# The second layer's token mixer on pairs of 2-byte floats in place of pairs of 4-byte floats

## The chip, the core and the metric

The kernel runs on one core of one Trainium2 chip. The core has five engines that each take their instructions from a queue of their own, in order: TensorE (PE in the profile, its weight loads PEld), VectorE (DVE), ScalarE (ACT), GpSimd (POOL) and SyncE (SP, which here only issues DMAs). They meet through semaphores. Operands of a matmul come from SBUF (128 partitions), its result goes to PSUM, which has eight banks of 128 x 512 4-byte floats. The metric is the time of one execution on the device in microseconds (us); the median of several runs counts.

## What is computed

Two layers of an encoder, 1024 tokens of 1024 numbers. Each layer normalises its input, shifts and scales it by a conditioning vector, runs a token mixer, adds the gated result, and then does the same with a squared-ReLU MLP. Layer 0's mixer is a latent attention. Layer 1's mixer, the one that the change touches, is a dilated sliding-window attention in three groups of 16 heads of 64:

```python
proj = (h @ w_in).reshape(B, S, 3, 3, 16, 64)          # group, (q k v), head
for gi, (window, dilation) in enumerate(((128, 1), (512, 4), (2048, 16))):
    q = rms_norm(proj[:, :, gi, 0], g_q[gi])
    k = rms_norm(proj[:, :, gi, 1], g_k[gi])
    v = proj[:, :, gi, 2]
    s = q @ k.T * 64 ** -0.5 + bias_table[bucket]       # |i - j| <= window / 2, same residue mod dilation
    o, lse = softmax(s) @ v, logsumexp(s)
wts = softmax(stack(lses), axis=0)                      # over the three groups
y = (sum over groups of wts * o) @ w_o
```

Everything is 4-byte float in the reference.

## The kernel before

**Products of pairs.** The kernel holds each operand of these products as a sum of two numbers, a high part and a low part, and a product is three matmuls: high by high, high by low, low by high (`mm3`, L504 to L506). There are two kinds of pair. `split` (L133, L134) makes two 4-byte numbers (written as fp32r): ACT copies the source into the high part, DVE takes source minus high. `parts` (L148, L151) makes two 2-byte floats: ACT writes the scaled source into the high part, DVE the rest, and that instruction also sums the rest over each row into a column of the tile `seen`. Before the change the two MLPs use `parts`, both mixers `split`.

**The range check.** 2-byte floats hold a small range of sizes, so `seen` collects the sums, and `floor` adds sums of a first tile that must not be too small; `fold` reduces `seen` once after each MLP and `verdict` compares at the end. `program` then runs the whole kernel a second time, on 4-byte pairs throughout (`half` false), if the comparison fails. `hs`, `ws`, `us` and `ys` are powers of two by which h, the weights, the MLP's hidden values and the gate are scaled.

**Layer 1's mixer.** `dil_v` first computes v for all three groups, by blocks in seven products in place of eight; its matmuls write the tile psv and have 512 columns. Then `dil` runs 96 steps, 32 for each group, four for each pair of heads. A step on PE is, in this order: products of q and k for two tiles of 128 queries (`products`, L2013, tile pss; two heads run side by side on 64 rows each); 24 projection matmuls for q and k of one token tile (psproj, 256 columns, `project`); four transposes (`stacks`, L1988, psq); 24 more; and the products of weights and v for two tiles (`av`, L2086 and L2087, psav). v is in three 2-byte parts of 64 columns, the weights of the softmax in two, so a key block costs one matmul of 192 columns and one of 128; groups 0 and 1 have two key blocks for each tile and head, group 2 one.

Around them, for the step just projected: `qkstep` squares (ACT, dsq), sums (DVE, dms), takes a reciprocal root (`rstd`, L124 to L128, ending in dry), multiplies (DVE, qn) and applies the gains (POOL, L1979). Two steps later PE transposes qn and ACT and DVE make the pair kT out of the bank (L1992, L1993). One step after that come the products; DVE adds the bias (L2029), ACT exponentiates (L2035) and makes the high part ph (L2072), DVE or POOL the low part (L2073), SP issues a DMA that transposes both into pT (L2074), and one step later `av` uses pT; DVE adds the three parts of the result into U (L2088). `v_parts` (L1959 to L1962) makes the three parts of v: ACT the first, DVE the rest, POOL the second and third. In group 2 the results of the three groups are merged as well (DVE and POOL, L2157, L2159), transposed, split and stored to a scratch tensor in DRAM, oTd. Before groups 1 and 2 `permute` copies h into the group's order.

Then `proj_res` multiplies with w_o (tile psy, 512 columns) and adds the residual.

**What sets the order.** The program is written in the order above; a scheduler with a model of the engines then orders each queue, and inside `dil` PE's order is held as written. Tiles come from pools of equal buffers (`G`: 29 buffers of 4 KB a partition; `X`: 20 in this layer; `sm`: six of each small size; eight PSUM banks), and a tile whose buffer is still read waits.

Of the kernel before, what the change touches and what calls it, by code (L numbers as in the profile page):

```python
# [41 lines left out]
class K:  # L42
    def __init__(self, ctx, tc, a, half, ng=29):
# [4 lines left out]
        self.hs, self.ws, self.us = (16.0, 512.0, 2.0 ** -10) if half else (1.0, 1.0, 1.0)  # L48
        self.ys = 2.0 ** -15 if half else 1.0
        self.cp = ctx.enter_context(tc.tile_pool(name="const", bufs=1))  # L50
# [6 lines left out]
        if half:  # L57
            misc = self.C("misc", [P, 8])
            self.bad, self.ones_y = misc[:, 0:4], misc[:, 4:5]
# [36 lines left out]
    def DR(self, shape, name):  # L96
        return self.dp.tile(list(shape), F32, name=self.pre + name)


    def setup(self):  # L100
# [6 lines left out]
        if self.half:  # L107
            nc.vector.memset(self.ones_y, self.ys)
        self.mods = {}
# [8 lines left out]
    def rstd(self, ms, n, name):  # L118
# [5 lines left out]
        nc.scalar.activation(l, ms, AF.Ln, bias=self.eps)  # L124
        nc.scalar.activation(y, l, AF.Exp, scale=-0.5)
        nc.vector.scalar_tensor_tensor(t, ms, EPS, y, op0=ALU.add, op1=ALU.mult)
# [9 lines left out]
    def pair(self, alloc, name, shape):  # L136

        if self.half:
            g = alloc(name, (shape[0], 2) + tuple(shape[1:]), F16)
            return g[:, 0], g[:, 1]  # L140
        return tuple(alloc(name + k, shape) for k in "hl")
# [12 lines left out]
    def seen_open(self):  # L154

        if self.half:
            self.seen, self.nseen, self.nlow = self.G("seen", (P, 512), F32), 0, 508
# [8 lines left out]
    def fold(self, k):  # L166

        tr, s = self.nc.vector.tensor_reduce, self.seen
        tr(self.bad[:, k : k + 1], s[:, 0 : self.nseen], op=ALU.add, axis=AX.X, apply_absolute_value=True)
        tr(self.bad[:, k + 2 : k + 3], s[:, 509 : self.nlow + 1], op=ALU.min, axis=AX.X)  # L170

    def verdict(self):

        nc = self.nc
        self.fold(1)
        t, m = self.sm("verdict", 4), self.sm("verdict", 1)
        nc.vector.tensor_scalar(t[:, 0:2], self.bad[:, 0:2], 512.0, None, op0=ALU.is_le)
        nc.vector.tensor_scalar(t[:, 2:4], self.bad[:, 2:4], 128.0, None, op0=ALU.is_ge)
# [41 lines left out]
    def consts(self, psp):  # L220
# [7 lines left out]
        if self.half:  # L228
            b = self.colc[:, 0:96].rearrange("p (l x) -> p l x", l=2)[:, :, 24:32]
            nc.gpsimd.tensor_scalar(b, b, self.hs, 1.0, op0=ALU.mult, op1=ALU.mult)  # L230
            g = self.colc[:, 112:128]
            nc.gpsimd.tensor_scalar(g, g, self.hs, 1.0, op0=ALU.mult, op1=ALU.mult)
# [55 lines left out]
    def ada_col(self, l, s, c, n, ps):  # L288
# [7 lines left out]
        if s == 3 and self.half:  # L296
# [12 lines left out]
    def ada_end(self, l, s, acc, row, psp, tag):  # L309
# [3 lines left out]
        if s % 3 == 2:  # L313
            for h in range(2):
                ps, c = PS(), slice(h * 512, (h + 1) * 512)
                if s == 5 and self.half:
# [91 lines left out]
    def h_store(self, Hh, d, x, mods, act=False, alloc=None, pin=False, keep=None):  # L408
# [3 lines left out]
        if d % 2 == 0:  # L412
            for k in range(2):
                Hh[k].append((alloc or self.G)(f"hT{k}", (P, 2, 512)))
# [12 lines left out]
        self.split(Hh[0][d // 2][:, d % 2, :], Hh[1][d // 2][:, d % 2, :], t)  # L427

    def h_steps(self, xs, mods, alloc=None, halloc=None, pin=False, act=False, keep=None):
# [5 lines left out]
        for d in range(ND):  # L435
            steps.append(lambda psp, tag, d=d: self.h_store(Hh, d, self.xT(xh, d, psp, tag), mods(), act=act or pin and d % 2 == 0,
                                                            alloc=halloc, keep=keep))
# [76 lines left out]

    def wsplit(self, src, shape, name, row=None, gain=None, alloc=None):

        nc = self.nc
        raw = self.load(src, shape, name + "r")
        hi, lo = ((alloc or self.G)(name + k, shape) for k in "hl")
        if row is not None:  # L520
            nc.gpsimd.tensor_tensor(raw, raw, row, op=ALU.mult)
        if gain is not None:
            nc.scalar.activation(hi, raw, AF.Copy, scale=gain)
            nc.vector.scalar_tensor_tensor(lo, raw, gain, hi.bitcast(F32), op0=ALU.mult, op1=ALU.subtract)
        else:
            self.split(hi, lo, raw)
        return hi, lo

# [537 lines left out]
    def reload(self, O, src, pp, th, eng=None):  # L1066
# [1466 lines left out]
```

## Time and profile before

| | |
|---|---|
| median of 3 runs | 3170.82 us (3169.37 to 3176.19) |
| the profiled execution | 3175.89 us |
| its span, first to last instruction | 3174.0 us |
| granted clock of PE, mean | 0.987 |
| v projection of layer 1 (`dil_v`) | from about 1390 to 1635 us of the span |
| the loop of `dil`, groups 0, 1, 2 | from about 1635, 1900 and 2180 us to about 2460 |
| output projection of layer 1 | from about 2460 to 2585 us |
| MLPs | from about 820 to 1390 and from 2585 to the end |

A row of a group of instructions names the line, the engine, the operation, what it writes and what it reads (`out<-in`, buffer numbers left out), partitions x elements and type, and the count; after the bar come the time that the group was busy, the mean of one in ns, and the idle time of the engine just before, with what ended it. "f32" stands for 4-byte operands, the pairs of `split` among them. A row of the order of time has the start and the length in us. A row of a table of stretches has the stretch, its length, each engine's busy time with its count, the granted clock, the DMA share and GB/s.

### The profile page before, as it was taken

What the parts mean: (1) busy time and instruction counts of PE and PEld (TensorE: products, weight loads), DVE (VectorE), ACT (ScalarE), POOL (GpSimd) and SP (SyncE); (2) the same over time, 40 slices, a digit from 0 to 9 for tenths busy, and PEclk for the clock granted to TensorE, in tenths of its full rate; (3) what the DMA queues carried; (4) which work ended last, traced back from release to release, by engine and by line L of the source; (5) the groups of instructions that cost most, each with busy time, mean ns of one, the idle gap of its engine ahead of it and who ended that gap; (6) DMA issues with size and microseconds to landing.
All of it is one profiled execution on the core that took longest, in us unless ns stands there. A gap on an engine that the chain in (4) does not pass through costs nothing. (4 is left out here: it accounts for less than half of the span.)

```text
span 3174.0 us, 51216 instructions
## 1 busy us (share of the span) xinstructions
PE 3072.2 (97%) x18036; PEld 2165.6 (68%) x18036; DVE 2385.7 (75%) x4734; ACT 1726.4 (54%) x3507; POOL 918.5 (29%) x1228
## 2 busy tenths in 40 slices
PE   6999999999999999999999999999999999999998
PEld 6877677778444444457889998999999764444443
DVE  5677777756998876688757778778787689779665
ACT  5547777863545543443226677668565355555441
POOL 7454655630011100001124445444454001110010
PEclk8999999999999999999999999999999999999999
DMA  5352332244665679555637887878776747438653
GB/s 196 110 184 83 108 98 97 71 137 133 215 227 181 240 233 298 190 190 178 212 118 188 181 180 174 193 186 173 168 177 163 217 134 249 163 136 289 226 198 94
DMA packets 540027, 554.53 MB, mean 175 GB/s; under 512 B 199493, under 2 KB 421106, under 8 KB 539754
## 3 DMA queue, kind: packets, MB, share of 16 engines
q1 hardware_dynamic: 501962, 445.10, 49.1%
q0 software_dynamic: 27360, 91.31, 7.8%
q10 hardware_dynamic: 10432, 14.68, 1.6%
q8 instruction: 146, 2.39, 0.3%
q14 instruction: 127, 1.04, 0.1%
HBM read 378.27 MB, written 132.62 MB: 161 GB/s over the span
## 5 line engine op out<-in xcount | busy, mean ns | idle before, releaser
L504 PE MATMUL psm<-hf,wf 128*128 128x512 f16 x896 | 340.8, 380 | 5.1 <-ACT wf L148 5.1
L505 PE MATMUL psm<-d,d 128*128 128x512 f16 x896 | 340.4, 380 | 4.7 <-DVE d L151 4.7
L505 PE MATMUL psm<-hf,wf 128*128 128x512 f16 x896 | 341.1, 381 | 0.0
L506 PE MATMUL psm<-d,d 128*128 128x512 f16 x896 | 340.3, 380 | 0.0
L506 PE MATMUL psm<-hf,wf 128*128 128x512 f16 x896 | 335.4, 381 | 4.7 <-DVE wf L151 4.6
L504 PE MATMUL psm<-d,d 128*128 128x512 f16 x896 | 334.7, 380 | 0.3 <-ACT d L148 0.3
L504 PE MATMUL psproj<-wqkh,hTp 128*128 128x256 f32 x1024 | 304.2, 297 | 0.0
L505 PE MATMUL psproj<-wqkl,hTp 128*128 128x256 f32 x1024 | 292.1, 285 | 0.0
L506 PE MATMUL psproj<-wqkh,hTp 128*128 128x256 f32 x1024 | 291.7, 285 | 0.0
L148 ACT ACTIVATE d<-ufr 128x1024 f16<-128x1024 f32 x112 | 117.8, 1052 | 206.2 <-PE psm L506 172.2
L504 PEld LDWEIGHTS psproj<-wqkh,hTp 128*128 128x128 f32 x1024 | 198.8, 194 | 9.0 <-issue 1.6
L505 PEld LDWEIGHTS psproj<-wqkl,hTp 128*128 128x128 f32 x1024 | 199.1, 194 | 0.2 <-DVE wqkl L134 0.2
L506 PEld LDWEIGHTS psproj<-wqkh,hTp 128*128 128x128 f32 x1024 | 198.5, 194 | 0.0
L151 DVE SCALAR_TENSOR_TENSOR d<-ufr,d 128x1024 f16<-128x1024 f32 x112 | 136.7, 1220 | 80.7 <-ACT d L148 80.5
L835 DVE TENSOR_REDUCE mx<-pmx 128x1 f32<-128x512 f32 x256 | 165.0, 682 | 27.9 <-PE pmx L833 27.7
L134 POOL TENSOR_TENSOR pl<-p,ph 128x1024 fp32r<-128x1024 f32 x58 | 141.3, 2436 | 138.4 <-ACT ph L133 128.2
L947 ACT ACTIVATE p<-pss 128x512 f32<-128x512 f32 x256 | 144.5, 589 | 51.7 <-PE pss L934 50.6
L1979 POOL TENSOR_TENSOR qn<-qn,dgain 128x256 f32<-128x256 f32 x96 | 89.8, 935 | 285.2 <-DVE qn L1977 238.3
L2035 ACT ACTIVATE pd<-pd,dnb 128x192 f32<-128x192 f32 (+2 forms) x384 | 167.7, 438 | 3.7 <-ACT dnb L2033 2.1
L2088 DVE TENSOR_REDUCE U<-psav 128x128 f32<-128x384 f32 x192 | 103.1, 551 | 86.4 <-PE psav L2087 86.1
L506 PEld LDWEIGHTS <-wf 128*128 128x128 f16 x896 | 88.0, 98 | 114.4 <-DVE wf L151 9.0
L504 PEld LDWEIGHTS <-wf 128*128 128x128 f16 x896 | 87.9, 98 | 113.6 <-ACT wf L148 9.6
(428 smaller groups left out, 8805.5 us busy)
## 6 DMA issues: line engine op xcount, KB each, us to landing
ufr<-uf SPq DMA_DIRECT2D x112, 512.0 KB
adaw<-in_ada_w SPq DMA_DIRECT2D x96, 512.0 KB
w2r<-in_mlp_w SPq DMA_DIRECT2D x96, 512.0 KB
w1r<-in_mlp_w SPq DMA_DIRECT2D x64, 512.0 KB
bt<-bias SPq DMA_DIRECT2D x128, 256.0 KB
wqkr<-in_dil_w_in SPq DMA_DIRECT2D x96, 256.0 KB
wvr<-in_dil_w_in SPq DMA_DIRECT2D x34, 512.0 KB
qkv<-st SPq DMA_DIRECT2D x32, 512.0 KB
```

The costliest lines, as they stand in the source:

```text
L134: return (lo_eng or nc.vector).tensor_tensor(lo, src, hi.bitcast(F32), op=ALU.subtract)
L148: nc.scalar.activation(hi, src, AF.Copy, scale=scale)
L151: return nc.vector.scalar_tensor_tensor(lo, src, scale, hi, op0=ALU.mult, op1=ALU.subtract, accum_out=self.seen[:, self.nseen - 1 : self.n ...
L504: mm(out, lh, rh, start=first, stop=False)
L505: mm(out, lh, rl, start=False, stop=False)
L506: mm(out, ll, rh, start=False, stop=last)
L835: nc.vector.tensor_reduce(maxes[h][:, 2 * j + b : 2 * j + b + 1], ps, op=ALU.max, axis=AX.X)
L947: nc.scalar.activation(p[:, b * 512 : (b + 1) * 512], ps[b], AF.Exp)
L1979: nc.gpsimd.tensor_tensor(qq, qq, gain[:, g : g + 1, :].unsqueeze(1).broadcast_to([P, 2, 2, 64]), op=ALU.mult)
L2035: nc.scalar.activation(p[:, e, lo:hi], p[:, e, lo:hi], AF.Exp, bias=nb[:, e : e + 1], accum_out=stat[:, g, t, 1, 2 * pr + e : 2 * pr + e + 1])
L2088: nc.vector.tensor_reduce(u["U"][:, t, :].rearrange("p (e d) -> p e d", e=2), ps[:, 0:384].rearrange("p (e k d) -> p e d k", e=2, k=3), op ...
```

## The change

In layer 1's mixer every `split` becomes a `parts`: h and its sums (hT, hs, hk), the weights wv, wqk and wo, the merged result oT; the pair kT is made on 2-byte floats too, scaled by 64, and v becomes a pair in place of three parts. Products keep their count but for `av`, whose matmuls have 128 and 64 columns in place of 192 and 128. The scales move through the mixer: h by 16, weights by 512, scores by 4096 (bias table and exponentials follow), gates by 2^-15. A pair lies in one buffer of `G` or `X` where two were needed, oTd has half the bytes, and `permute` copies 2-byte numbers. The range check grows: `seen` is opened three times and folded three times, `floor` looks at five first tiles more, and for the norms three small instructions on POOL add up the fourth power of dry in a tile `most`. Layer 0's mixer stays as it was.

```diff
@@ wo_form (w_form, dil_weights.split, h_form, h_store alike)
-        hi, lo = (self.G("wo" + k, (P, 2, 512)) for k in "hl")
-        self.split(hi, lo, raw)
+        half = self.half and self.layer == 1
+        hi, lo = self.pair(alloc or self.G, "wo", (P, 2, 512), half)
+        (self.parts(hi, lo, raw, self.ws) if half else self.split(hi, lo, raw))
@@ v_parts
-            vs = D_("vs", (P, 2, 4, 192), BF16, 8)
+            vs = D_("vs", (P, 2, 4, 128 if self.half else 192), F16 if self.half else BF16, 8)
...
+            if self.half:
+                self.held(lambda: self.parts(v4[:, :, 0:64], v4[:, :, 64:128], p4, 2.0 ** -7))
+                for i in range(n):
+                    VS[t + i] = vs[:, i]
+                return
@@ qkstep
-            r = self.rstd(ms, 8, "dr")
+            r = self.rstd(ms, 8, "dr", self.half)
+            if self.half:
+                y4 = self.sm("y4", 8)
+                nc.gpsimd.tensor_tensor(y4, r, r, op=ALU.mult)
+                nc.gpsimd.tensor_tensor(y4, y4, y4, op=ALU.mult)
+                nc.gpsimd.tensor_tensor(most, most, y4, op=ALU.add)
@@ stacks
-            nc.scalar.activation(hi, x, AF.Copy)
-            nc.vector.tensor_tensor(lo, x, hi.bitcast(F32), op=ALU.subtract)
+            if self.half:
+                nc.scalar.activation(hi, x, AF.Copy, scale=64.0)
+                nc.vector.scalar_tensor_tensor(lo, x, 64.0, hi, op0=ALU.mult, op1=ALU.subtract)
...
@@ av
+                    if self.half:
+                        o = ps[:, e * 128 : (e + 1) * 128]
+                        c = slice((n * e + b) * P, (n * e + b + 1) * P)
+                        nc.tensor.matmul(o, pT[:, 0, c], v, start=b == 0, stop=False)
+                        nc.tensor.matmul(o[:, 0:64], pT[:, 1, c], v[:, 0:64], start=False, stop=b == n - 1)
+                        continue
...
+            k = 2 if self.half else 3
             nc.vector.tensor_reduce(u["U"][:, t, :].rearrange("p (e d) -> p e d", e=2),
-                                    ps[:, 0:384].rearrange("p (e k d) -> p e d k", e=2, k=3), op=ALU.add, axis=AX.X)
+                                    ps[:, 0 : 128 * k].rearrange("p (e k d) -> p e d k", e=2, k=k), op=ALU.add, axis=AX.X)
@@ dil
-        oTd = self.DR([6, 2, P, 2, 512], "oTd")
+        oTd = self.DR([6, 2, P, 2, 512], "oTd", F16 if self.half else F32)
...
-                                      "k": D_("kT", (P, 2, S + 512), F32R, 2), "U": self.G("U", (P, 8, P), F32)}
+                                      "k": D_("kT", (P, 2, S + 512), self.DT, 2), "U": self.G("U", (P, 8, P), F32)}
@@ run
+        k.layer = 1
+        k.seen_open()
         vd = k.DR([3, S, D], "v")
...
         O, first, banks = k.dil(at, at1, tail, wqk, vd)
+        k.fold(1)
+        k.seen_open()
```

How the queues stand at three places. First PE, at the end of a step of group 1, where weights (pT) are multiplied with v (vs). Before:

```order
L2086 LDWEIGHTS pT_23655
L2086 MATMUL psav_23884<-vs_22802,pT_23655 128x192
L2087 LDWEIGHTS pT_23655
L2087 MATMUL psav_23884<-vs_22802,pT_23655 128x128
L2086 LDWEIGHTS pT_23655
L2086 MATMUL psav_23884<-vs_22942,pT_23655 128x192
```

And after the change:

```order
L2109 LDWEIGHTS pT_23640
L2109 MATMUL psav_23868<-vs_22777,pT_23640 128x128
L2110 LDWEIGHTS pT_23640
L2110 MATMUL psav_23868<-vs_22777,pT_23640 128x64
L2109 LDWEIGHTS pT_23640
L2109 MATMUL psav_23868<-vs_22918,pT_23640 128x128
```

The sequence and the number of weight loads are the same; the columns are fewer. Second DVE, in a step of group 2 in which v is split and weights are split (wqk): from the end of the bias additions to the two reductions of U. Before:

```order
L126 SCALAR_TENSOR_TENSOR drt_31781<-dms_31776,dry_31779 128x8
L127 SCALAR_TENSOR_TENSOR drt_31781<-drt_31781,dry_31779 128x8
L134 TENSOR_TENSOR wqkl_31797<-wqkr_31279,wqkh_31796 128x1024
L128 SCALAR_TENSOR_TENSOR dry_31779<-drt_31781,dry_31779 128x8
L134 TENSOR_TENSOR wqkl_31801<-wqkr_31571,wqkh_31800 128x1024
L1977 TENSOR_TENSOR qn_31787<-psproj_31707,dry_31779 128x512
L1960 TENSOR_TENSOR vr_31791<-vraw_31385,vs_31790 128x512
L1993 TENSOR_TENSOR kT_31391<-psq_31869,kT_31391 128x2x256
L2088 TENSOR_REDUCE U_30835<-psav_31900 128x128
L2088 TENSOR_REDUCE U_30835<-psav_31906 128x128
```

And after the change:

```order
L133 SCALAR_TENSOR_TENSOR drt_31847<-dms_31842,dry_31845 128x8
L158 SCALAR_TENSOR_TENSOR vs_31860,seen_18958<-vraw_31446,vs_31860 128x8x64
L134 SCALAR_TENSOR_TENSOR drt_31847<-drt_31847,dry_31845 128x8
L158 SCALAR_TENSOR_TENSOR wqk_31863,seen_18958<-wqkr_31336,wqk_31863 128x1024
L135 SCALAR_TENSOR_TENSOR dry_31845<-drt_31847,dry_31845 128x8
L158 SCALAR_TENSOR_TENSOR wqk_31866,seen_18958<-wqkr_31636,wqk_31866 128x1024
L1995 TENSOR_TENSOR qn_31857<-psproj_31773,dry_31845 128x512
L2012 SCALAR_TENSOR_TENSOR kT_31452<-psq_31934,kT_31452 128x2x256
L2117 TENSOR_REDUCE U_30885<-psav_31965 128x128
L2117 TENSOR_REDUCE U_30885<-psav_31971 128x128
```

The same work stands between the bias additions and kT; the rest of v has moved ahead of the weights. Third POOL, in group 2: the gains (qn), the low parts of the weights (ph) and, after the change, the three additions for the norms (y and most). Before:

```order
L1979 TENSOR_TENSOR qn_31382<-qn_31382,dgain 128x2x128
L2073 TENSOR_TENSOR ph_31407<-pd_31421,ph_31407 128x256
L1979 TENSOR_TENSOR qn_31530<-qn_31530,dgain 128x2x128
L2073 TENSOR_TENSOR ph_31547<-pd_31551,ph_31547 128x256
L2073 TENSOR_TENSOR ph_31547<-pd_31561,ph_31547 128x256
```

And after the change:

```order
L1997 TENSOR_TENSOR qn_31443<-qn_31443,dgain 128x2x128
L2095 TENSOR_TENSOR ph_31468<-pd_31482,ph_31468 128x256
L1990 TENSOR_TENSOR y_5847_31591<-dry_31583 128x8
L1991 TENSOR_TENSOR y_5847_31591<-y_5847_31591 128x8
L1992 TENSOR_TENSOR most<-most,y_5847_31591 128x8
L2095 TENSOR_TENSOR ph_31612<-pd_31616,ph_31612 128x256
L1997 TENSOR_TENSOR qn_31595<-qn_31595,dgain 128x2x128
L2095 TENSOR_TENSOR ph_31612<-pd_31626,ph_31612 128x256
```

The low part ph of the next step's first tile stands behind three instructions that wait for that step's dry.

164 lines of the change are left out of this document (96 added, 68 removed).

## The prediction

> **What bounds the kernel now.** I read the page first, then a table of stretches, then the order of time on PE. Every time of matmuls in a row below is a latency of some 0.2 to 0.4 us; matmuls overlap, so what counts is the distance between two starts.
>
> ```profile
> span 3174.0 us, 51216 instructions
> PE 3072.2 (97%) x18036; PEld 2165.6 (68%) x18036; DVE 2385.7 (75%) x4734; ACT 1726.4 (54%) x3507; POOL 918.5 (29%) x1228
> 1390.00:1635.00 245.00, 241.04 (x1083) 196.24 (x1082) 188.27 (x213) 69.75 (x79) 26.64 (x51) 1.00 0.53 178
> 1635.00:1900.00 265.00, 260.92 (x2440) 250.65 (x2440) 196.25 (x538) 175.92 (x504) 110.64 (x127) 1.00 0.75 176
> 1900.00:2200.00 300.00, 291.81 (x2739) 279.50 (x2738) 234.12 (x655) 216.31 (x619) 140.77 (x196) 0.99 0.80 182
> 2200.00:2460.00 260.00, 250.16 (x2217) 239.25 (x2216) 208.53 (x604) 156.56 (x524) 128.30 (x146) 0.97 0.74 170
> 1975.00:2109.00 134.00, 134.00 (x1276) 129.21 (x1276) 100.27 (x290) 90.68 (x274) 59.82 (x88) 1.00 0.83 190
> 2254.00:2391.00 137.00, 133.30 (x1187) 127.52 (x1186) 114.74 (x330) 83.84 (x284) 70.38 (x81) 0.97 0.74 170
> ```
>
> The stretches give their length, then the busy time of PE, PEld, DVE, ACT and POOL, the granted clock, the DMA share and GB/s. The first is the v projection (dil_v), the next three the loop of dil, group by group, and the last two are 16 steps each inside group 1 and group 2. PE never pauses in group 1 (134.00 of 134.00: 8.38 us a step); in the last third 10 of 260 us are open. DVE is at 75% in group 1 and at 84% in group 2. So a step of dil is as long as its matmuls, and what shortens matmuls shortens the step until another engine's 84% becomes 100%.
>
> **The price of a matmul.** The first and last start of a run of 21 psproj matmuls (4-byte, 256 columns), of 16 of the MLP (2-byte, 512), of 15 of psv (4-byte, 512), and three starts of psav (2-byte):
>
> ```profile
> 2000.64 0.28 PE L504 MATMUL psproj<-wqkh,hTp 128*128 128x256 f32 x1
> 2003.03 0.28 PE L506 MATMUL psproj<-wqkh,hTp 128*128 128x256 f32 x1
> 2799.64 0.38 PE L505 MATMUL psm<-hf,wf 128*128 128x512 f16 x1
> 2802.88 0.38 PE L505 MATMUL psm<-hf,wf 128*128 128x512 f16 x1
> 1539.68 0.39 PE L504 MATMUL psv<-wvh,hsh 128*128 128x512 f32 x1
> 1542.86 0.39 PE L506 MATMUL psv<-wvh,hsl 128*128 128x512 f32 x1
> 2006.61 0.25 PE L2086 MATMUL psav<-vs,pT 128*128 128x192 bf16 x1
> 2006.69 0.22 PE L2087 MATMUL psav<-vs,pT 128*128 128x128 bf16 x1
> 2007.44 0.25 PE L2086 MATMUL psav<-vs,pT 128*128 128x192 bf16 x1
> ```
>
> That is 2.39/20 = 119.5 ns, 3.24/15 = 216.0, 3.18/14 = 227.1, and six psav pairs in 0.83, 138.3 ns a pair. A 2-byte line through 512 columns at 216.0 and the pair's mean (160 columns at 69.2) has 0.417 ns a column and 2.5 ns fixed: 109.2 at 256, 55.9 at 128, 29.2 at 64. So 4-byte operands cost 10.3 ns more at 256 and 11.1 at 512.
>
> **The change, part by part.** The counts:
>
> ```profile
> 1634.00:1900.00 266.00, 199.13 (x1536) 187.62 (x1536) 21.39 (x31) 18.92 (x32) 1.00 0.76 176
> 1900.00:2200.00 300.00, 212.66 (x1637) 200.16 (x1638) 23.45 (x34) 20.02 (x34) 0.99 0.80 182
> 2200.00:2470.00 270.00, 192.83 (x1437) 181.28 (x1435) 21.37 (x31) 17.72 (x30) 0.96 0.75 176
> 1390.00:1635.00 245.00, 232.39 (x1008) 188.28 (x1008) 54.26 (x84) 6.94 (x12) 1.00 0.53 178
> 2460.00:2600.00 140.00, 94.59 (x384) 72.23 (x384) 10.64 (x16) 0.98 0.57 166
> L2086 PE MATMUL psav<-vs,pT 128*128 128x192 bf16 x640 | 101.9, 251 | 12.9 <-DMA pT<-ph 12.8
> L2013 PE MATMUL pss<-kT 64*128 64x256 f32 x1152 | 99.3, 303 | 11.4 <-DVE kT L1993 7.8 <-DVE U L2088 3.4 <-ACT kT L1992 0.3
> ```
>
> The first five are stretches of psproj (three), psv and psy alone. (A) psproj: 96 steps of 48 are 4608 matmuls (the stretches count two twice), times 10.3 ns: 47.5 us. (B) psv, 1008 times 11.1: 11.2 us. (C) the output projection, 384 times 11.1: 4.3 us. (D) psav: 640 pairs of 192 and 128 columns become 128 and 64. The 128 costs 55.9. No row has 64 columns: at least the line's 29.2, at most the 55.9 of the shortest matmul that loads weights, so a pair saves 53.2 to 26.5 ns, 34 to 17 us. The ends are near each other and no row is nearer to one; I take the middle, 25. (E) pss: two heads run side by side, 576 such pairs of 256 columns; between nothing and A's 10.3 ns, 0 to 5.9 us; the columns are A's, so 6. A to E are **94 us**, all of it on the engine that sets the end.
>
> The Trainium skill, "TensorE: Matmul & The Clock Gate", section "Back-to-back issue gap", gives two rules for such streams: a column time plus 2.5 ns, and sustained figures with weight loads of about 81 ns at 128 columns and 131 at 512. By the second, D would turn round: two matmuls of 81 against 138.3 a pair, some 15 us lost in place of 25 won, 54 in all and 3131 us after the losses below, outside the range. The trace has 80 ns for 192 columns and 216 for 512; it bears out the first and refutes the second, which gets no chance of its own.
>
> What stands against it. On DVE:
>
> ```profile
> L2088 DVE TENSOR_REDUCE U<-psav 128x128 f32<-128x384 f32 x192 | 103.1, 551 | 86.4 <-PE psav L2087 86.1
> L1973 DVE TENSOR_REDUCE dms<-dsq 128x8 f32<-128x512 f32 x96 | 64.9, 676 | 11.8 <-ACT dsq L1972 11.7
> L151 DVE SCALAR_TENSOR_TENSOR d<-ufr,d 128x1024 f16<-128x1024 f32 x112 | 136.7, 1220 | 80.7 <-ACT d L148 80.5
> L151 DVE DVE_READ_ACCUMULATOR d<-ufr,d 128x1 f32 x112 | 9.2, 82 | 0.0
> L134 DVE TENSOR_TENSOR wqkl<-wqkr,wqkh 128x1024 fp32r<-128x1024 f32 x48 | 64.4, 1341 | 4.4 <-ACT wqkh L133 1.8 <-issue 1.3 <-PE psproj L505 0.4
> 2251.38 0.38 PE L2013 MATMUL pss<-kT 64*128 64x256 f32 x2
> 2253.33 1.01 PE L2013 MATMUL pss<-kT 64*128 64x256 f32 x10 [1.57 <-DVE kT L1993]
> 2254.27 0.58 PE L504 MATMUL psproj<-wqkh,hTp 128*128 128x256 f32 x1
> ```
>
> The reduction of U reads 256 in place of 384 numbers; 676 and 551 lie 128 apart, so it drops 125 ns, 4.1 us of the 33 in the group-2 stretch. A split by parts (1220) costs no more than the split it replaces (1341); with its 82 ns read of the accumulator, 24 times there, I put +2. DVE needs 112.6 us where PE now wants 137 less half of group 2's share of the sum: A 15.8 (32 of 96 steps), D 5 (128 of 640 pairs), E 2, together 23. So DVE would be busy 112.6 of 125.5, 90%. Its work is bunched: every eighth step kT's low part comes late and the products wait (the last three rows), PE 1.95 us behind. That wait is DVE's and will not shrink with PE, so about a third of the 23 is lost: **-8**, between 0 and -23. Where PE waits so long its clock drops: 0.97 in the last third is 7 to 8 us of 260, and it stays in the times above.
>
> In groups 0 and 1 DVE stays near 80%. DMA moves the same bytes (bias, raw weights, raw v) except oTd: 0.83 of 134 is 111 us in a stretch that would take 120, 93%. Transposes of pT queue behind bias loads there: **-5**, between 0 and -15. ACT's instructions stay the same in number and shape, and it is at 68%.
>
> POOL loses two instructions for each of 56 v pieces and gains three of 8 numbers in each of 96 steps:
>
> ```profile
> L1961 POOL TENSOR_SCALAR vs<-vr 128x512 bf16<-128x512 f32 x48 | 44.3, 924 | 20.1 <-PE pss L2013 13.2 <-DVE vr L1960 6.9
> L1962 POOL TENSOR_TENSOR vs<-vr,vs 128x512 bf16<-128x512 f32 x48 | 60.4, 1260 | 2.8
> L597 POOL TENSOR_TENSOR qrw<-st,sin 128x64 f32<-128x64 f32 x32 | 10.3, 321 | 0.0
> 2305.31 1.23 SPq L2074 DMA_TRANSPOSE pT<-ph  x1
> 2311.27 0.26 PE L2086 MATMUL psav<-vs,pT 128*128 128x192 bf16 x1
> ```
>
> At no more than 0.32 us each (the nearest row has 64 columns) they add at most 1 us a step, under 93 in all, beside 105 us that go, and POOL is at 45%: nothing, since neither sum is on PE's path. The three wait for dry, the end of a chain on DVE; in group 2 they stand ahead of a ph, which the transpose needs. The cover is the 6.0 us from a transpose's issue to its psav. The folds and floors are some ten DVE reductions under 0.7 us, in dil_v and the projection, where DVE is at 77%: -1. Weight and h pairs take one buffer for two; I count nothing for it.
>
> Sum: 94 - 8 - 5 - 1 = **80 us**. The profiled execution took 3175.89 us around its span of 3174.0, 5 above the median 3170.82; taken from the median, 80 leaves **3091 us**.
>
> **The rivals.** (1) DVE and DMA take over: group 2 gains nothing (-15 beyond forecast); groups 0 and 1 stop at a DMA share of 0.90, 111/0.90 = 123.6 us for 16 steps, 10.4 a stretch or 42 of their 57, (-10 beyond); the clock in group 2 falls to 0.94 (-8): 47 left, 3124. For it: 84% and 0.83 already; against: not one gap in group 1. (2) Everything is kept: D at 34, no loss on DVE or DMA, and half of PE's 10 open us in the last third closed since POOL disturbs DVE less: 94 + 9 + 5 = 108, 3063. (3) The 10 ns are not the data type's but those of PE's 256 columns with ever new weights: A and E vanish, 40 less 5, 3136. Against it: the same 11 at 512 columns. (4) **Slower**: in group 2 POOL holds ph until dry, a whole step (7.1 us) late. The landing takes at least the 1.23 us that its issue lasts; I count 2 of the 6.0 us cover for it, so from 4 us on PE waits, here 3.1 us in each of 32 steps, 99 us, and 80 less 99 makes 3190. For it: the order puts them so; against: only one ph of two, and not in every step. (5) A check of the ranges fails and the whole 4-byte program runs after it: over 6200.
>
> **How the numbers follow.** Forecast 0.55, (1) 0.18, (2) 0.13, (3) 0.05, (4) 0.04, (5) 0.02, and 0.03 that gains and new waits cancel within 0.2% (6 us, about what a measurement of this kernel can tell from no change). Faster: 0.55 + 0.18 + 0.13 + 0.05 = 0.91; same 0.03; slower 0.06. The range holds the forecast's own bounds (D, DVE, DMA: 3074 to 3112), (1) and most of (2): 3064 to 3126; (3), (4), (5) and no change stay out.
>
> **What would show it.** A and E: starts of psproj 0.109 us apart and steps of group 1 of 7.5 us in place of 8.38. D: psav pairs 0.085 to 0.112 apart. B: dil_v 11 us shorter. The losses: the open time of PE in group 2 about doubles, with kT, U or pT named ahead of it, and more of it under half clock. I am wrong in kind if psproj stays at 0.12 us, or if psav waits for pT in most steps; wrong in size if steps of group 1 shrink by less than 0.6 us or those of group 2 as much as PE's own sum, 0.7.

## The result and the profile after

The changed kernel takes 3115.93 us (median of 4 runs, 3112.99 to 3128.26) against 3172.02 of the kernel before (4 runs): a ratio of 0.9829, 95% interval 0.9801 to 0.9858. So 56 us are gained where 80 were forecast. The profiled execution of the changed kernel took 3128.26, 12 above the median, at a mean granted clock of 0.980 where the other three had 0.984 (0.4% of its 3126 us is 12.5), and its profile is compared with that of before as it stands.

The head of its page, two stretches of 140 and 165 us inside groups 0 and 1 and one of 185 us in group 2, the columns as in the prediction:

```profile
span 3126.4 us, 51410 instructions
PE 2972.7 (95%) x18036; PEld 1884.6 (60%) x18036; DVE 2334.8 (75%) x4936; ACT 1707.1 (55%) x3507; POOL 866.7 (28%) x1409
1690.00:1830.00 140.00, 135.88 (x1473) 117.17 (x1470) 107.79 (x349) 104.60 (x311) 52.26 (x106) 0.98 0.82 204
1935.00:2100.00 165.00, 157.65 (x1714) 136.86 (x1712) 121.98 (x415) 121.93 (x372) 65.73 (x155) 0.99 0.83 200
2200.00:2385.00 185.00, 172.00 (x1750) 148.25 (x1748) 159.92 (x525) 123.23 (x423) 98.25 (x166) 0.99 0.72 158
```

PE, which never paused in group 1, is now open for 7.35 of 165 us. No other engine is full: DVE is at 74% in group 1 and at 86% in group 2, and the DMA share is 0.83, what it was before.

**The matmuls are cheap as forecast, and more.** One step of group 1 that waits for nothing, in the order of time: the starts of the first two pairs of psav, the first pss, the first two psproj of the step, the four psq in its middle with the psproj behind them, and the first psproj of the next step.

```profile
1938.67 0.22 PE L2109 MATMUL psav<-vs,pT 128*128 128x128 f16 x1
1938.75 0.22 PE L2109 MATMUL psav<-vs,pT 128*128 128x128 f16 x1
1939.44 0.83 PE L2035 MATMUL pss<-kT 64*128 64x256 f16 x12
1940.21 0.28 PE L517 MATMUL psproj<-wqk,hTp 128*128 128x256 f16 x1
1940.33 0.27 PE L518 MATMUL psproj<-wqk,hTp 128*128 128x256 f16 x1
1942.84 0.60 PE L2006 MATMUL psq<-ident,qn 128*128 128x128 f32 x4
1943.27 0.27 PE L517 MATMUL psproj<-wqk,hTp 128*128 128x256 f16 x1
1947.43 0.28 PE L517 MATMUL psproj<-wqk,hTp 128*128 128x256 f16 x1
```

From psproj to psproj the step takes 7.22 us, where it took 8.41. The same places before:

```profile
1998.06 0.26 PE L2086 MATMUL psav<-vs,pT 128*128 128x192 bf16 x1
1999.27 0.98 PE L2013 MATMUL pss<-kT 64*128 64x256 f32 x12
2000.18 0.39 PE L504 MATMUL psproj<-wqkh,hTp 128*128 128x256 f32 x1
2000.40 0.28 PE L505 MATMUL psproj<-wqkl,hTp 128*128 128x256 f32 x1
2003.15 0.60 PE L1988 MATMUL psq<-ident,qn 128*128 128x128 f32 x4
2003.50 0.36 PE L504 MATMUL psproj<-wqkh,hTp 128*128 128x256 f32 x1
2003.70 0.28 PE L505 MATMUL psproj<-wqkl,hTp 128*128 128x256 f32 x1
```

The products with v went from 1.21 us (1998.06 to 1999.27) to 0.77, the scores from 0.91 to 0.77, the 48 projections (the rest of a step: 8.41 and 7.22 less these) from 5.94 to 5.25; the four psq grew from 0.35 to some 0.43. In group 2, with half the products with v, an undisturbed step is 6.88 in place of 7.86.

**And the waits are new.** The longest waits of PE in the loop of dil (us in all, times, the longest one) of before:

```profile
PE psav L2086 <- DMA pT<-ph: 12.8, 8, 3.0
PE pss L2013 <- DVE kT L1993: 7.8, 9, 1.9
PE pss L2013 <- DVE U L2088: 3.4, 1, 3.4
```

and of the changed kernel:

```profile
PE psav L2109 <- DMA pT<-ph: 32.0, 15, 6.7
PE pss L2035 <- DVE kT L2012: 20.8, 16, 3.5
PE pss L2035 <- ACT kT L2011: 8.1, 9, 2.2
```

To see where, I count for stretches of steps (numbered from 0; a step begins with its first psproj, and the loop ends with the first psy) the time from the first step's beginning to the end of the last, less the steps at their undisturbed length. For steps 38 to 59 of the changed kernel the two psproj are at 1932.98 and 2101.86: 168.9 us, less 22 times 7.22, is 10.0 lost.

| steps | what is there | lost before | lost after |
|---|---|---|---|
| 8 to 27, 38 to 59 | inside groups 0 and 1 | 0.9 and 0.0 | 8.3 and 10.0 |
| 28 to 37, 60 to 69 | the two turns | 9.3 and 12.6 | 24.0 and 27.8 |
| 70 to 93 | inside group 2 | 16.6 | 22.0 |
| 94 and 95 | the end of the loop | 7.3 | 21.5 |
| the whole loop | 830.0 us before, 790.1 after | 40.2 | 107.9 |

(The first eight steps, which lack some of a step's work, gain 6 us against the rule in both.) Undisturbed steps fell by 107.6 us in all, and 67.7 of these came back. The whole loop as one stretch, before and after:

```profile
1634.85:2464.86 830.01, 804.54 (x7409) 770.76 (x7409) 643.91 (x1804) 552.34 (x1659) 381.81 (x472) 0.99 0.77 177
1632.07:2422.16 790.09, 720.58 (x7410) 614.07 (x7408) 593.96 (x1933) 536.35 (x1659) 325.85 (x650) 0.95 0.78 185
```

PE is idle for 25.5 us before and 69.5 after, 44 more. Most of the rest came back as half clock behind the waits: the granted clock is 0.986 and 0.953 in three digits, which is at most 12 us of the loop before and 37 after (at most, since PE is idle in part of it). Where these waits come from is the question for the experiments. Each loss below is read from one profiled execution; run 3, which takes away small instructions on POOL alone, differs from the changed kernel by up to 2.5 us in a stretch.

### The profile page after: what moved, and what is told of

It is laid out like the page before. It is cut to its first block, busy times and chain, and to the rows that moved or that the text cites. A ratio compares the mean times of both kernels' runs of the same rounds, so it can differ in the third digit from the quotient of the medians.

```text
span 3126.4 us, 51410 instructions
## 1 busy us (share of the span) xinstructions
PE 2972.7 (95%) x18036; PEld 1884.6 (60%) x18036; DVE 2334.8 (75%) x4936; ACT 1707.1 (55%) x3507; POOL 866.7 (28%) x1409
## 5 line engine op out<-in xcount | busy, mean ns | idle before, releaser
L517 PE MATMUL psproj<-wqk,hTp 128*128 128x256 f16 x1024 | 287.7, 281 | 0.0
L518 PE MATMUL psproj<-wqk,hTp 128*128 128x256 f16 x1024 | 286.9, 280 | 0.0
L519 PE MATMUL psproj<-wqk,hTp 128*128 128x256 f16 x1024 | 286.8, 280 | 0.0
L519 PEld LDWEIGHTS <-wf 128*128 128x128 f16 x896 | 87.8, 98 | 118.6 <-DVE wf L158 14.0
L517 PEld LDWEIGHTS <-wf 128*128 128x128 f16 x896 | 87.8, 98 | 114.8 <-ACT wf L155 12.1
L519 PEld LDWEIGHTS <-d 128*128 128x128 f16 x896 | 87.8, 98 | 110.6 <-issue 5.8
L517 PEld LDWEIGHTS <-d 128*128 128x128 f16 x896 | 87.9, 98 | 106.3 <-issue 1.9
L518 PEld LDWEIGHTS <-d 128*128 128x128 f16 x896 | 87.8, 98 | 106.0 <-issue 1.7
L518 PEld LDWEIGHTS <-wf 128*128 128x128 f16 x896 | 87.8, 98 | 104.1 <-issue 0.7
L141 DVE TENSOR_TENSOR pl<-p,ph 128x1024 fp32r<-128x1024 f32 x70 | 93.8, 1341 | 72.8 <-ACT ph L140 65.9
```

The costliest lines, as they stand in the source:

```text
L141: return (lo_eng or nc.vector).tensor_tensor(lo, src, hi.bitcast(F32), op=ALU.subtract)
L517: mm(out, lh, rh, start=first, stop=False)
L518: mm(out, lh, rl, start=False, stop=False)
L519: mm(out, ll, rh, start=False, stop=last)
```

## The experiments

All times are medians; the kernel before ran beside them at 3173 to 3175. Edits are against the changed kernel unless another is named.

**1. Spread the loads of v.** Every eighth step of groups 0 and 1 is long, and there SP issues up to seven loads of v; this is one such place (SP's queue, then DVE):

```profile
1972.27 0.52 SPq L1946 DMA_DIRECT2D vraw<-v  x1
...
1976.12 1.83 SPq L1951 DMA_DIRECT2D vraw<-v  x1
1978.23 0.39 SPq L2046 DMA_DIRECT2D bt<-bias  x1
...
1979.94 3.16 SPq L2096 DMA_TRANSPOSE pT<-ph  x1
1980.86 0.36 DVE L2051 CUSTOM_DVE_ANT_0 pd<-pss,bt 128x192 f32<-128x192 f32 x1 [2.63 <-DMA bt<-bias]
```

```diff
-vtodo.setdefault(n - 4, []).append(VS["load"])
...
+for k in range(3):
+    vtodo.setdefault(n - (4 if late else 6) + k, []).append(lambda k=k, load=load: load(k))
```

> The changed kernel, with the loads of raw v for the next four heads issued two or three a step over three steps, in place of all (seven in group 1) at the start of one step. Theory (order of SP): in every eighth step of groups 0 and 1 the bias load stands behind these issues, so the products of weights and v wait 1.1 to 2.3 us for pT and run at half clock after. Then those waits go, steps 8 to 27 and 38 to 59 lose under 3 us each against 7.22 a step where they lose 8.3 and 10.0, and the median falls from 3116 by 12 to 20 us, to 3096 to 3104. Rival (DMA is full): the same bytes give the same waits, 3112 to 3120.

Measured: 3118.88 (ratio 0.9822, 0.9806 to 0.9837), no gain; steps 8 to 27 lose 6.3, 38 to 59 lose 9.9. The waits did not go, they moved two steps ahead, with the loads: now the transpose itself is held.

```profile
1956.14 4.78 SPq L2097 DMA_TRANSPOSE pT<-ph  x1
1955.00:1965.00 10.00, 8.51 (x97) 7.08 (x94) 6.51 (x23) 6.20 (x20) 3.07 (x10) 1.00 1.00 222
```

In these 10 us the DMA share is 1.00, and the transpose takes 4.78 us to issue, where the median of steps 8 to 59 of the changed kernel is 1.63 (and the longest 4.61). So the order of the issues on SP alone is not the cause; what the DMA engines have to do is left, and run 5 tries it. The Trainium skill, "Trainium Kernel Development and Optimization", section "Key Constraints", says that DMAs of all queues run on the same 16 engines; this run agrees, for loads and transposes of one queue alone.

**2. Spread the copies of permute** over the last eight steps of a group, one eighth each (the pairs leave buffers free for it).

```diff
-if step is not None and step[1] < 2 and step[2] == 7 and step[3] >= 2:
...
+if self.half and step is not None and step[1] < 2 and step[2] >= 6:
...
+    permute(*perms.pop(0))
+elif step is not None and step[1] < 2 and step[2] == 7 and step[3] >= 2:
```

> The changed kernel, with the copies that permute h made one eighth a step over the last eight steps of a group, in place of one eighth, two eighths and the rest at the turn. Theory (the turns are paced by bunched copies on ACT and DVE, PE's saving is lost there): steps 28 to 37 and 60 to 69 lose 10 to 15 us each where they lose 24.0 and 27.8, median 3085 to 3098. Rival (the turn is paced by the weights' loads and the chain from projection to products, which the copies only sit beside): the turns lose 20 or more each as now, 3108 to 3120.

Measured: 3111.54 (0.9803, 0.979 to 0.9816), which the interval does not part from the changed kernel. The turns lose 7.6 and 18.9 in place of 24.0 and 27.8, where 10 to 15 each were expected; but steps 8 to 27, in the last four of which copies now run, lose 15.7 in place of 8.3, and group 2 25.2 in place of 22.0. So the copies have a large part in what the turns lose, but little is won by moving them: the turns lose 25 less, and the median falls by 4.

**3. Without the sums on POOL.**

```diff
-    nc.gpsimd.tensor_tensor(y4, r, r, op=ALU.mult)
-    nc.gpsimd.tensor_tensor(y4, y4, y4, op=ALU.mult)
-    nc.gpsimd.tensor_tensor(most, most, y4, op=ALU.add)
```

> The changed kernel without the three small instructions on POOL in each step that add up the fourth power of dry; the tile most stays at zero, so the range check no longer looks at the norms. Theory (POOL's additions are covered, as the prediction said): 3112 to 3120, and the losses at turns and in every eighth step stay. Rival (they hold the gains of qn and the low part of ph behind dry, and what is lost at the turns and at the end is theirs): the loss of the two turns and of steps 94 and 95, 73 us now, falls by 15 or more, 3090 to 3104.

Measured: 3117.64 (0.9819, 0.9804 to 0.9834). Turns and end lose 21.5, 25.4 and 20.5, 67 in place of 73: the sums are covered, the rival is out.

**4. The spread loads of v in the kernel before** (the edit of run 1).

> The kernel before, with the spread of the loads of raw v of e1_v_spread. Theory: before, a step of 8.41 us of matmuls covered the late bias load, so there was nothing to win, 3168 to 3176, and the lost time of steps 8 to 27 and 38 to 59 stays at about 1 and 0 us. Rival (the spread helps by itself, whatever PE does): 10 us or more faster, under 3162.

Measured: 3193.92, 0.7% slower (1.0069, 1.0056 to 1.0083). Inside groups 0 and 1 nothing was lost, as expected (1.4 and 1.6); the first turn lost 14.2 in place of 9.3 and group 2 27.9 in place of 16.6. I had expected no change there. Run 1 has the same in group 2 (32.8 in place of 22.0), so this cost does not come from the faster matmuls, and it may hide what run 1 won in the turns (they lose 19.9 and 22.9 there). Buffers held two steps longer would explain it, which was not tried.

**5. and 6. The bias loaded once for a pair of heads**, in the changed kernel and in the kernel before.

```diff
-if g < 2 or t % 2 == 0:
+if t == 0:
     u["bias"] = D_("bt", (P, 2, 256), F32, 3)
...
+if t == 0 or g == 2 and t == 1:
     nc.sync.dma_start(out=bt, in_=src.rearrange("o h (q c) -> q (o h) c", c=256)[:, :, b0:b1])
```

> The changed kernel, with the bias of a pair of heads loaded once for all eight tiles of 128 queries; the reload for each tile, needed only where the positions are not evenly spaced, is left out. It takes away 512 KB a step (7 of 8) in groups 0 and 1 and leaves every instruction of PE, DVE, ACT and POOL as it is. Theory (the transposes of pT and the loads queue in the DMA engines; spreading the issues could not help, bytes do): the waits of psav for pT in every eighth step go, steps 8 to 27 and 38 to 59 lose under 3 us each where they lose 8.3 and 10.0, the turns lose some less, median 3088 to 3104. Rival (the lost time is the chain of DVE, ACT and POOL between projection and pT, whatever the DMAs do): 3112 to 3120 and the same losses.

> The kernel before, with the bias loaded once for a pair of heads as in e5_bias_once. Theory: before, PE's 8.41 us a step covered the DMAs, so steps 8 to 27 and 38 to 59 have nothing to win (they lose 0.9 and 0.0), only the turns and group 2 some: 3160 to 3174. Rival (the bias loads cost time in any case): as much faster as e5 against the changed kernel, 3145 to 3158.

Measured: 3094.72 (0.9753, 0.9738 to 0.9768) for the changed kernel, 21 us faster; 3167.28 (0.9981, 0.9973 to 0.999) for the kernel before, 6 us faster. A stretch of 140 us inside group 0, as above for the changed kernel, and the waits of psav:

```profile
1690.00:1830.00 140.00, 136.81 (x1515) 119.66 (x1513) 112.05 (x361) 110.18 (x326) 55.25 (x111) 1.00 0.68 154
PE psav L2110 <- DMA pT<-ph: 26.4, 13, 5.1
```

The DMA share falls from 0.82 to 0.68. Steps 8 to 27 and 38 to 59 lose 3.6 and 4.7 in place of 8.3 and 10.0, a little more than the 3 expected, and the turns and the end 19 less together. In the kernel before these steps lost nothing and gain nothing. So inside groups 0 and 1 the same DMAs cost time only beside the faster matmuls; but 26 of 32 us of waits for pT remain, and bytes are only part of the answer. In the whole loop PE's idle time falls by 13 us only (69.5 to 56.5), while the granted clock rises from 0.953 to 0.980, at most 22 us (some 12 of these may belong to the one profiled execution of the changed kernel): with fewer waits the clock stays up.

**7. The parts of the weights in two steps.**

```diff
-if n in loads:
-    self.held(lambda: wts.update({firsts[n][0:3]: loads.pop(n)()}))
+for m, k in ((n + 1, 0), (n, 1)):
+    if m in loads:
+        self.held(lambda: wts.setdefault(firsts[m][0:3], []).append(loads[m](k)))
```

> The changed kernel, with the two buffers of weights of a pair of heads made into parts in two steps, one each, the second in the step that first needs it, in place of both in the step before. Theory (in group 2 the low part of kT waits behind merge and 2.4 us of weight parts on DVE in every fourth step): steps 70 to 93 lose 14 to 18 us where they lose 22.0, median 3108 to 3113. Rival (DVE's sum sets group 2, or the second half comes late for the first products): no gain or a loss, 3115 or more.

Measured: 3112.26 (0.9806, 0.9789 to 0.9822). Group 2 loses 26.0, more than the 22.0; that theory falls for group 2. Steps 38 to 59 lose 4.7 in place of 10.0, steps 8 to 27 10.6 in place of 8.3.

**8. v in three parts again.**

```diff
-vs = D_("vs", (P, 2, 4, 128 if self.half else 192), F16 if self.half else BF16, 8)
+vs = D_("vs", (P, 2, 4, 192), BF16, 8)
...
-nc.tensor.matmul(o[:, 0:64], pT[:, 1, c], v[:, 0:64], start=False, stop=b == n - 1)
+nc.tensor.matmul(o[:, 0:128], pT[:, 1, c], v[:, 0:128], start=False, stop=b == n - 1)
```

> The changed kernel with v in three 2-byte parts again (192 and 128 columns in av, two more instructions on POOL for each piece of v, a reduction of U over 384): one part of the change undone. It gives PE 34.8 us of work back (64 steps at 0.434 us, 32 at 0.221). Theory (where the loop waits for DMAs and DVE, PE's time is not what counts): the end comes 12 to 24 us later, 3128 to 3140, and the losses of every eighth step and of the turns shrink. Rival (PE sets the end throughout and the waits come on top): 30 us or more, 3146 to 3152.

Measured: 3147.94 (0.9917, 0.9903 to 0.9931), 32 us slower for 34.8 us of PE. This is the rival's number and spoke against my theory. But the edit also gives DVE and POOL their work back, and at its own undisturbed steps (7.65 us, in group 2 7.10) the loop loses 100.9, with steps 8 to 27 and 38 to 59 at 9.4 and 7.6. So the next two runs give PE's time back alone.

**9. and 10. PE's time put back, and nothing else.**

```diff
 def project(h, w, ps, i, t):
...
+    for _ in range(5 if self.half else 0):
+        nc.tensor.matmul(ps[:, i * 256 : (i + 1) * 256], h[t // 4](0, 0)[:, tl], w[0][0][:, 0, :], start=True, stop=True)
```

(2 in place of 5 in run 10.)

> The changed kernel with PE's time put back and nothing else: ten more matmuls of 256 columns in each step outside the turns (five ahead of each projection, overwritten by the first real product), 92 steps times 1.09 us, 100 us. A step is then 8.31 us, next to the 8.41 of the kernel before. Theory (waits that a step of 8.4 us covered came into view because PE is faster): the losses of steps 8 to 27 and 38 to 59 fall from 8.3 and 10.0 to 2 or less and those of the turns and of group 2 by 5 to 12 each, so the median rises by only 45 to 70, 3161 to 3186. Rival (the waits belong to the changed kernel's own order and come on top of PE, as the run with v in three parts gave 32 of its 35 us): 85 or more, 3201 or later.

> The same with four such matmuls in each step, 92 times 0.437 us, 40 us: PE's time as with v in three parts, without that kernel's extra work on DVE and POOL. Theory (uncovered waits): 12 to 28 us later, 3128 to 3144, and fewer waits in the eighth steps than with v in three parts, whose own instructions made new ones. Rival (PE's time counts in full between waits): 35 or more, 3151 or later.

Measured: 3165.72 (0.9975, 0.9965 to 0.9985) with ten, 50 us for 100; 3130.63 (0.9868, 0.985 to 0.9886) with four, 15 us for 40. With four, the steps are as long as in run 8 (7.66 us in groups 0 and 1), but steps 8 to 27 and 38 to 59 lose 3.6 and 3.7 where run 8 lost 9.4 and 7.6: bare PE time brings fewer waits than the parts of v did, as expected. With ten, in a stretch of 180 us of group 1, and all waits of psav and the longest of pss in the loop:

```profile
1960.00:2140.00 180.00, 179.74 (x1944) 158.20 (x1942) 125.48 (x411) 123.95 (x375) 67.97 (x157) 1.00 0.78 189
PE psav L2111 <- DMA pT<-ph: 4.8, 3, 3.4
PE pss L2037 <- DVE kT L2014: 18.5, 12, 2.8
```

PE is full again. Steps 8 to 27 and 38 to 59 lose 0.4 and 0.1, the turns 12.8 and 13.1, group 2 15.6, the end 6.2: 42.3 in the whole loop where the kernel before lost 40.2. The granted clock of the loop is 0.990. With the changed kernel's own POOL sums, parts and order all in place, the waits are those of before as soon as a step is as long as before. This settles it: the 67.7 us are not made by the change's other work, they are waits, and half clock behind waits, that PE's time had covered.

**11. Faster still: two products in place of three** in the projections of q and k.

```diff
-self.mm3(ps[:, i * 256 : (i + 1) * 256], h[t // 4](0, d)[:, tl], h[t // 4](1, d)[:, tl],
+self.mm2(ps[:, i * 256 : (i + 1) * 256], h[t // 4](0, d)[:, tl], h[t // 4](1, d)[:, tl],
...
+    self.nc.tensor.matmul(out, lh, rh, start=first, stop=False)
+    self.nc.tensor.matmul(out, lh, rl, start=False, stop=last)
```

> The changed kernel without the third product (low part of h by high part of the weights) in the projections of q and k: 16 of 48 psproj matmuls of each step are left out, 96 times 1.75 us, 168 us of PE. Theory (DMAs, turns and DVE set more and more of the loop as PE gets faster): at most half arrives, 40 to 85 us, 3031 to 3076, with DVE at 95% or more in group 2. Rival (PE sets the pace of most steps still): 120 or more, under 2996.

Measured: 3102.64 (0.9788, 0.9771 to 0.9805): 13 us for 168, far less than under either theory. Two stretches, 130 us of group 0 and 180 us of group 2, and what PE waits for in the loop:

```profile
1690.00:1820.00 130.00, 100.97 (x1050) 81.66 (x1048) 99.59 (x320) 95.40 (x284) 50.48 (x97) 0.93 0.77 199
2190.00:2370.00 180.00, 134.00 (x1260) 107.35 (x1261) 150.61 (x487) 110.83 (x385) 90.55 (x154) 0.90 0.69 154
PE psav L2115 <- DMA pT<-ph: 112.6, 52, 8.2
PE pss L2041 <- DVE kT L2018: 50.9, 32, 6.0
```

PE is at 78 and 74%, DVE at 77 and 84, DMA at 0.77 and 0.69: nothing is full, and the loop is no shorter than 764 us. By these waits, what sets it is the row of work between two products of PE: every second step waits for pT, which comes from scores over bias, exponential, parts and a DMA, and is due one step later. That one engine should reach 95% was wrong.

**12. Four changes together:** the bias once (positions that are not evenly spaced go to the second program), the copies spread, the weights' parts in two steps, and the output weights earlier.

```diff
+nc.vector.tensor_tensor(m[0:1], m[0:1], self.flf, op=ALU.mult)
...
-if step[1:3] == (2, 7):
-    tail(tp)
+if step[1] == 2 and step[2] >= 6:
+    tail(4 * (step[2] - 6) + tp)
```

> The changed kernel with four changes together: the bias of a pair of heads loaded once on the fast path (positions that are not evenly spaced now fail the range check and run the second program), the copies of permute spread over eight steps, the weights of q and k made into parts in two steps, and the output weights loaded and made into parts over six steps from pair 6 of group 2 on, in place of the last four. Theory: the gains alone were 21, 4 and 4 us, and the last two steps lose 8 less; together 3075 to 3092. Rival (they free the same time): no better than the bias alone, 3092 or more.

Measured: 3097.17 (0.976, 0.9744 to 0.9776). Faster than both kernels, with nothing left out, but no better than the bias alone. The earlier output weights did what was expected (the last two steps lose 6.4 in place of 21.5), and the copies moved the turns' loss again (8.0 and 16.4) into steps 8 to 27 (15.6) and 38 to 59 (12.4), group 2 losing 30.9.

## Why the prediction's range held and its terms did not

The forecast of 3091 was 25 us too low. The range 3064 to 3126 held, but the forecast's own bounds of 3074 to 3112 did not (all of D, DVE and DMA at their ends would be 3069 to 3124): the range was wide enough because it had to hold rival 1, and because two errors ran against each other, which is luck. Both sides of the sum were too small: 94 us of gain were 123 (the 107.6 of the loop, and B and C as priced), and of these 75 were lost, not 14: the spans of the profiled pair are 47.6 apart (the medians 56, so a usual execution loses some 8 less).

| | of PE's undisturbed steps, us each | steps | sum |
|---|---|---|---|
| A, psproj | 0.69 | 96 | 66 |
| D, psav | 0.434, in group 2 0.221 | 64, 32 | 35 |
| E, pss | 0.149 | 96 | 14 |
| psq | -0.08 | 96 | -8 |

The terms, the forecast of each in brackets:

- **A (47.5).** The price in a run was right: starts lie 0.109 us apart, as forecast. What was missed is in the rows of before quoted above: the first 4-byte matmul behind pss held the next for 0.22 us and the first behind psq for 0.20, where others take 0.12. Behind psq 0.08 of this is no loss: there the last psq takes 0.03 us where it takes 0.11 now, which is the row psq of the table. Behind pss 0.10 us a step remain, 10 us in all. I had measured 21 starts inside a run and left out its first.
- **D (25, between 17 and 34).** The upper end: 0.434 us for 8 pairs is 54 ns a pair. The first pair above takes 0.08 (1938.67 to 1938.75). The rule of the Trainium skill, "TensorE: Matmul & The Clock Gate", section "Back-to-back issue gap" (column time plus 2.5 ns, given there for a matmul by itself), makes it an estimated 85 ns a pair. The trace agrees, in a stream with weight loads too. The prediction had the same line from its own rows and should have followed it down to 64 columns.
- **E (6, bounds 0 to 5.9).** 14, beyond the upper bound, and for the same reason as A. The first pair of pss starts at 1999.27 before and at 1939.44 after; rows of narrow windows begin with the second and the third pair:

```profile
1999.49 0.40 PE L2013 MATMUL pss<-kT 64*128 64x256 f32 x4
1999.61 0.40 PE L2013 MATMUL pss<-kT 64*128 64x256 f32 x4
1939.56 0.38 PE L2035 MATMUL pss<-kT 64*128 64x256 f16 x4
1939.67 0.49 PE L2035 MATMUL pss<-kT 64*128 64x256 f16 x6
```

  The first pair held the next for 0.22 us and now does for 0.12; a later pair went from 0.12 to 0.11 (medians over the steps 8 to 27, 38 to 59 and 70 to 92 in which pss did not wait: 223 and 119 ns, 119 and 109). So the price within the run is that of psproj, some 5 us as bounded, and the other 10 us are again the start of a 4-byte run. That one cost, two places a step and some 20 us in all, is what A and E left out.
- **B (11.2) and C (4.3).** The price held (15 psv take 3.24 us, from 1539.96 to 1543.20, 0.216 each), but less than half of B arrived: from the first psv to the first psproj it is 238.4 us in place of 242.9. PE waited longer for the low parts of the weights there (the groups of psv with most idle time, after and before):

```profile
L518 PE MATMUL psv<-wv,hs 128*128 128x512 f16 x240 | 93.2, 389 | 7.2 <-DVE wv L158 7.2
L505 PE MATMUL psv<-wvl,hsh 128*128 128x512 f32 x239 | 93.5, 391 | 2.2 <-DVE wvl L134 2.2
```

  C's stretch, from the first psy to the first psm, fell by 8.1 (107.1 to 99.0; the last products of the attention lie in it too). In the first 100 us of the second MLP PE is busy for 91.0 us in place of 95.3, with DVE at 92 to 93 in both: some of the gain was given back there.

- **DVE in group 2 (-8):** measured 5.4 (22.0 less 16.6), and kT's low part is the wait, as forecast; DVE stands at 86%, not 90. The mean step of 70 to 93 fell by 0.75 us (8.55 to 7.80), which is the sign that the prediction gave for being wrong in size: PE's own saving there was not 0.7 but 0.98.
- **DMA in groups 0 and 1 (-5):** 17.4 (8.3 and 10.0, less 0.9). The mechanism was right, transposes of pT wait behind loads, and run 5 shows that bytes carry some 10 of it; the size was off by three.
- **The turns and the end (nothing):** 44 us (73.3 less 29.2). This is the term that failed. The prediction looked for an engine whose share would reach 100%, in two stretches of 16 quiet steps, and let every gain outside them pass in full. The turns were already long before the change: what is late there depends on DVE, ACT and the DMAs (the copies, run 2; the output weights at the end, run 12), and 1.19 us less of PE a step does not bring it sooner. And the prediction let the lost clock stay as it was: in the turns and the end PE's idle time grew from 18 to 45 us, and what half clock took from at most 7 to at most 31. Runs 9 to 11 show the rule that it used ("what shortens matmuls shortens the step until another engine's 84% becomes 100%") to be wrong here: no engine is full when PE has long stopped to set the time.
- **POOL (nothing)** was right (run 3), and rival 4 with it out: psav waits for pT 15 times in 96 steps, not for POOL's sums. Rival 3 is refuted by the 0.109. Rival 1 was nearest in size (3124), but of group 2, where it put the most, came the least of the new loss.

What one us of PE is worth, from runs 9 to 11, as the matmuls of an undisturbed step in groups 0 and 1 get shorter:

| | step, us | matmuls of the loop | loop | lost | median |
|---|---|---|---|---|---|
| kernel before | 8.41 | 789.8 | 830.0 | 40.2 | 3172.02 |
| ten more matmuls | 8.31 | 782.5 | 824.9 | 42.3 | 3165.72 |
| four more | 7.66 | 722.7 | 794.5 | 71.8 | 3130.63 |
| changed kernel | 7.22 | 682.2 | 790.1 | 107.9 | 3115.93 |
| two products | 5.47 | 514.2 | 764.2 | 249.9 | 3102.64 |

From 8.31 to 7.66 us 59% of the matmuls' saving arrives in the median (35.1 of 59.8 us), from there to 7.22 36% (14.7 of 40.5), below that 8% (13.3 of 168). By the intervals of the ratios each difference of medians is known to some 7 to 11 us, so the second share lies between about 10 and 60%; that the third is far below the first is sure. The removal of v's third part was worth 32 of 35 us (run 8), while 40 us of bare PE time are worth 15. At nearly the same steps the loop loses 100.9 us in run 8 and 71.8 in run 10, so the difference is in waits; that the third part's work on DVE and POOL makes them is likely, but it was not tried apart from where PE's time lies in the step.

## What to carry to other kernels

An engine that is busy all the time hides the waits of all others; before its work is made shorter, ask of each wait that ends just in time, and of the irregular places (turns, ends, bulk loads) first, how late it will be. Other engines' busy shares do not answer that, since a row of dependent work can set the time while every engine has room. A wait costs its own time and can cost half clock behind it, so both are to be counted. Matmuls that do nothing, added in steps, measure on the chip what the next microsecond saved is worth.

## What the runs showed of the hardware

A wait of PE of 2 us can halve its clock, and the same wait elsewhere does not. In the changed kernel, after a wait of 2.04 us a pair of psav takes 0.16 us (1985.53 to 1985.69). In run 5 a wait of 2.46 us is followed by pairs of 0.09 (1718.13 to 1718.22), at a clock of 1.00. The stretches are of 3.41 us, three around the first place and two at the second:

```profile
1985.31 0.23 PE L2109 MATMUL psav<-vs,pT 128*128 128x128 f16 x1 [2.04 <-DMA pT<-ph]
1985.53 0.29 PE L2109 MATMUL psav<-vs,pT 128*128 128x128 f16 x1
1985.69 0.29 PE L2109 MATMUL psav<-vs,pT 128*128 128x128 f16 x1
1982.03:1985.44 3.41, 1.37 (x15) 1.00 (x13) 1.75 (x4) 3.41 (x13) 1.32 (x4) 1.00 1.17 230
1985.44:1988.86 3.42, 3.42 (x33) 2.37 (x32) 2.35 (x9) 1.00 (x4) 1.44 (x3) 0.50 0.83 233
1988.86:1992.27 3.41, 3.41 (x33) 3.11 (x32) 1.71 (x9) 3.05 (x12) 1.32 (x4) 1.00 1.03 270
1718.13 0.23 PE L2110 MATMUL psav<-vs,pT 128*128 128x128 f16 x1 [2.46 <-DMA pT<-ph]
1718.22 0.22 PE L2110 MATMUL psav<-vs,pT 128*128 128x128 f16 x1
1716.38:1719.80 3.42, 1.67 (x30) 1.33 (x31) 1.12 (x3) 0.09 (x2) 0.77 (x1) 1.00 0.95 231
1719.80:1723.21 3.41, 3.41 (x33) 3.10 (x32) 2.61 (x13) 2.47 (x10) 1.19 (x4) 1.00 1.01 271
```

The Trainium skill, "TensorE: Matmul & The Clock Gate", section "What's actually happening", has the clock set by windows of some 3.4 us that run free of the program. The traces agree: in the loop of all fourteen profiled executions every stretch of half clock lasts 3.41 us or two or three times that, and within one execution they all start on one grid of 3.41 us. They also show what goes with it. The wait of 2.04 us lay in one window, which left PE idle for 2.04 of 3.41 us, and the next window was at half clock; the wait of 2.46 us lay across the border of two, idle for 0.72 and some 1.74. In the loops of the changed kernel and its ten variants 138 windows at full clock were followed by half clock, and PE was idle for 1.75 us or more in each; in the 2206 others it was idle for 1.93 us at most. (In the three profiles on the kernel before it was 1.57 or more against at most 1.63.) So a window about half idle is enough here, where the Trainium skill speaks of an idle one.

4-byte operands (fp32r) cost two things here: some 10 ns a matmul in a run (119.5 for 109.2 ns at 256 columns, 227.1 for 216.0 at 512, 119 for 109 a pair of pss), and some 0.10 us once where such a run begins behind other matmuls (0.22 us for 0.12, at the first pair of pss and at the first psproj behind pss). Behind the four psq nothing is lost.
